# Weight pages of 4608 bytes, with the split weights begun at another offset in each group of 512 columns

## The chip, the cores and the metric

The kernel runs on one core of a Trainium2 chip. The metric is the device time of one execution in microseconds (us). The kernel before was timed twice: 1624.48 and 1625.87 us, median 1625.17 us.

## What is computed

One layer of a streaming encoder on 256 tokens of width 2048, float32 throughout. Cut to what matters here:

```
xn = rms_norm(h)
proj = xn @ w_in            # z_a (u, v), q, c_kv, q_idx, k_idx, w_idx, gates
y_a = spatial_gating_unit(gelu(z_a))
y_b = indexer_sparse_attention(q, rms_norm(c_kv), q_idx, k_idx, w_idx, w_uk, w_uv)
mixed = g_a * (y_a @ w_oa) + g_b * (y_b @ w_ob)
h = h + mixed @ w_out
hn = rms_norm(h)
h = h + (silu(hn @ w_ff_gate) * (hn @ w_ff_up)) @ w_ff_down     # inner width 5632
return rms_norm(h)
```

Nearly all of the work is products of 256 tokens with weight matrices, some 300 MB of weights that are each read once.

## The kernel before, in words

**Weights.** Every weight matrix is cut into groups of 512 columns, and each group into chunks of two k tiles: 128 partitions by 1024 float32 numbers, 512 KB. `wchunk` (line 72) handles one chunk: SyncE (SP) loads it into a page `raw` (line 80), ScalarE (ACT) writes its upper mantissa bits to a page `wh` (line 67), and VectorE (DVE) writes the rest to a page `wl` (line 68). The pool `wp` (line 44) has four pages each of `raw`, `wh` and `wl`, 4096 bytes long in each partition; a chunk's matmuls free its `wh` and `wl` when they are through.

**Products.** A product in float32 is three passes: upper by upper, lower by upper, upper by lower. `nat_group` (line 89, with `mm3` at lines 84 to 87) makes `[tokens, 512]` blocks: the activations are the stationary operand (the weight load, PEld), and 512 columns of `wh` or `wl` stream past them as the moving operand. That is 12 matmuls of 512 columns to a chunk. The groups v, u, g (gates), oa, ob, out, vv, fg, fu and fd are made so: 488 chunks. `tr_group` (line 104, matmuls at lines 117, 119 and 120) has it the other way round: 128x128 pieces of `wh` or `wl` are the stationary operand and 256 tokens move, 24 matmuls to a chunk. The groups qi, q and k are made so: 56 chunks. The first product (kv, before any group) has 16 smaller chunks of 592 columns, read as two halves of 296 columns, b = 0 and b = 1, so that the second half begins 1184 bytes into the page.

**Order.** The groups run one after another in the order of the program: kv, qi0, qi1, v0 to v3, then four times q, k, vv, attention, u and a layer norm; gates and oa, gates and ob, out, and the feed-forward blocks fg and fu with the partial down products fd between them. A last part works from eight chunks of `fd` that stay split on chip (`kept_h`, `kept_l`; they lie in pages of the pool `tp`, not `wp`).

**Other pages.** The pool `np` (line 46) holds 11 pages `[128, 2, 512]` float32, 4096 bytes each: x, v, u, the layer norm's factors `gb`, gates, the residual `h`, the feed-forward's `s` and the final gain `fg` (the tile; the group of that name is the gate half of the feed-forward). A tile takes a page that an earlier tile has left, and the first instruction that writes it waits for the last that read the old one. The loads of `gb` (line 340), `h` (line 457) and `fg` (line 505) stand in SP's queue between the weight loads.

Of the kernel before, what the change touches and what calls it, by code (L numbers as in the profile page):

```python
# [30 lines left out]
KVW = LAT + IDXD + IDXH  # L31
NEG = -1.0e38
MARK = -3.0e38
WARM = 8  # matmuls of zeros that open the clock gate


@with_exitstack
def block_kernel(ctx: ExitStack, tc: tile.TileContext, a, out):
    """Every product against a weight matrix is float32 = three float32r passes: an operand is
    split exactly into h (its upper 12 mantissa bits, rounded) and l (the rest, 12 bits), and  # L40
    h*h + l*h + h*l is accumulated in float32."""
    nc = tc.nc
    const = ctx.enter_context(tc.tile_pool(name="const", bufs=1))
    wp = ctx.enter_context(tc.tile_pool(name="wp", bufs=4))
    tp = ctx.enter_context(tc.tile_pool(name="tp", bufs=24))
    np_ = ctx.enter_context(tc.tile_pool(name="np", bufs=11))
    sp = ctx.enter_context(tc.tile_pool(name="sp", bufs=1))
    acc_p = ctx.enter_context(tc.tile_pool(name="acc", bufs=4, space=bass.MemoryType.PSUM))
    aux_p = ctx.enter_context(tc.tile_pool(name="aux", bufs=4, space=bass.MemoryType.PSUM))
# [7 lines left out]
    def acc_tile(name):  # L57
        return acc_p.tile([P, 512], F32, tag="acc", name=name)
# [2 lines left out]
        return aux_p.tile([P, 512], F32, tag="aux", name=name)  # L61

    def split(h, l, src, scale=None):
        """h + l = src (times a scale per partition), exactly."""
        hf = h.bitcast(F32)
        if scale is None:
            nc.scalar.activation(h, src, AF.Copy)  # L67
            nc.vector.tensor_tensor(l, src, hf, op=ALU.subtract)  # L68
        else:
            nc.scalar.activation(h, src, AF.Copy, scale=scale)  # L70
            nc.vector.scalar_tensor_tensor(l, src, scale, hf, op0=ALU.mult, op1=ALU.subtract)

    def wchunk(src, cols, keep=False):
        raw = wp.tile([P, 1024], F32, tag="raw", name="raw")
        if keep:
            h, l = (t_tile(z).rearrange("p a b -> p (a b)") for z in ("kept_h", "kept_l"))
        else:
            h = wp.tile([P, 1024], F32R, tag="wh", name="wh")
            l = wp.tile([P, 1024], F32R, tag="wl", name="wl")
        nc.sync.dma_start(raw[:, :cols], src)  # L80
        split(h[:, :cols], l[:, :cols], raw[:, :cols])
        return h, l
# [4 lines left out]
        nc.tensor.matmul(o, ll, rh, start=False, stop=stop, **kw)  # L87

    def nat_group(w, ks, x, name):
        """[tokens, 512] blocks of x @ w for both token tiles. w: [chunks, 128, 1024] in DRAM;  # L90
        ks: its k tiles; x(k) -> the k tile's (h, l), [128, 256] each."""
        acc = [acc_tile(f"{name}_{t}") for t in range(2)]
        for c in range(len(ks) // 2):
            wh, wl = wchunk(w[c], 1024)
            for j in range(2):
                i = 2 * c + j
                xh, xl = x(ks[i])
                for t in range(2):
                    s = slice(t * P, (t + 1) * P)
                    mm3(acc[t], xh[:, s], xl[:, s], wh[:, j * 512:(j + 1) * 512],  # L100
                        wl[:, j * 512:(j + 1) * 512], i == 0, i == len(ks) - 1)
        return acc

    def tr_group(w, ks, x, name, bank=acc_tile, beside=None):
        """(x @ w).T for 512 columns of w: two banks of [128 columns, 2, 256 tokens]. beside(c) is
        called after each chunk."""
        acc = [bank(f"{name}_{b}").rearrange("p (c t) -> p c t", c=2) for b in range(2)]
        for c in range(len(ks) // 2):
            wh, wl = wchunk(w[c], 1024)
            for j in range(2):  # L110
                i = 2 * c + j
                xh, xl = x(ks[i])
                for ct in range(4):
                    s = slice(j * 512 + ct * P, j * 512 + (ct + 1) * P)
                    o = acc[ct // 2][:, ct % 2, :]
                    last = i == len(ks) - 1
                    nc.tensor.matmul(o, wh[:, s], xh, start=(i == 0 and ct % 2 == 0), stop=False,  # L117
                                     skip_group_check=True)
                    nc.tensor.matmul(o, wh[:, s], xl, start=False, stop=False, skip_group_check=True)  # L119
                    nc.tensor.matmul(o, wl[:, s], xh, start=False, stop=last, skip_group_check=True)  # L120
            if beside is not None:
                beside(c)
        return acc

    def rsqrt(dst, src, mul, add, m, name):
        """dst = 1 / sqrt(src * mul + add), [128, m]: Newton's steps from the bits' guess, each left
        with a factor (a power of two) that the last product takes out."""
        v = sp.tile([P, m], F32, tag=f"rs_v{m}", name=f"{name}_v", bufs=2)
        y = sp.tile([P, m], F32, tag=f"rs_y{m}", name=f"{name}_y", bufs=2)
        w = sp.tile([P, m], F32, tag=f"rs_w{m}", name=f"{name}_w", bufs=2)  # L130
        nc.vector.tensor_scalar(v, src, mul, add, op0=ALU.mult, op1=ALU.add)
        nc.vector.tensor_scalar(y.bitcast(I32), v.bitcast(I32), -0.5, 1597463007.0,
                                op0=ALU.mult, op1=ALU.add)
        for three in (3.0, 12.0, 768.0):
            if m == 1:
                nc.vector.scalar_tensor_tensor(w, y, y, v, op0=ALU.mult, op1=ALU.mult)
            else:
                nc.vector.tensor_tensor(w, y, y, op=ALU.mult)
                nc.vector.tensor_tensor(w, w, v, op=ALU.mult)
            nc.vector.scalar_tensor_tensor(y, w, three, y, op0=ALU.subtract, op1=ALU.mult)  # L140
        nc.vector.tensor_scalar(dst, y, -1.0 / 8192.0, None, op0=ALU.mult)

    def transposed(src, name, h, l, scale=None):
        """src [128 tokens, 2, 512] -> h, l [128, 4, 256 tokens]."""
        for b in range(2):
            pt = aux_tile(f"{name}_pt{b}").rearrange("p (c t) -> p c t", c=2)
            for c in range(2):
                for t in range(2):
                    ct = 2 * b + c
                    nc.tensor.transpose(pt[:, c, t * P:(t + 1) * P], src[:, t, ct * P:(ct + 1) * P], ident)  # L150
            if scale is None:
                split(h[:, 2 * b:2 * b + 2], l[:, 2 * b:2 * b + 2], pt)
            else:
                for c in range(2):
                    ct = 2 * b + c
                    split(h[:, ct], l[:, ct], pt[:, c], scale=scale[:, ct:ct + 1])

# [1 line left out]
    # while the first loads run: the activation table, and the tensor engine's clock  # L159
    warm = const.tile([P, 512], BF16, name="warm")  # L160
    nc.vector.memset(warm, 0.0)
    table = const.tile([P, 1], BF16, name="table")
# [27 lines left out]
    x_nat = a["x"].rearrange("(t p) (n c) -> n p t c", p=P, c=512)  # L190

    def sumsq(ss, src, n):
        """ss[:, n, t] = the sums of squares of src [128, 2, 512]'s rows."""
        for t in range(2):
            junk = sp.tile([P, 512], BF16, tag="junk", name="junk")
            nc.scalar.activation(junk, src[:, t], AF.Square, accum_out=ss[:, n, t:t + 1])
# [7 lines left out]

    ss1 = sp.tile([P, 4, 2], F32, name="ss1")

# [1 line left out]
    KS = list(range(KT))  # L208
    HW = KVW // 2
    kv = [[acc_tile(f"kv{b}{t}") for t in range(2)] for b in range(2)]  # L210
# [54 lines left out]
    def c_of(k):  # L265
        return cT_h[:, k], cT_l[:, k]

# [1 line left out]
    index_queries(1, acc_tile)  # L269
    cT_h, cT_l = t_tile("cT_h"), t_tile("cT_l")  # L270
    transposed(c_n, "cT", cT_h, cT_l, scale=gkv)
# [19 lines left out]

    for hp in range(8):
        score_pair(hp)
    # keep: 0 where a key is kept, else a large negative; [tile 1's 256 keys | tile 0's 128]
    keep = sp.tile([P, T + P], F32, name="keep")
    for t in (1, 0):
        w = (t + 1) * P
        nc.vector.memset(score[t][0:CHUNK, w - CHUNK:w], NEG)
        for i in range(TOPK // 8):
# [2 lines left out]
            nc.vector.match_replace(score[t], m8, score[t], MARK)  # L302
        nc.vector.tensor_scalar(keep[:, :T] if t else keep[:, T:], score[t], 0.5 * (NEG + MARK), -1.0e30,
                                op0=ALU.is_gt, op1=ALU.mult)
    # r1 * B_HEAD_DIM ** -0.5, for tile 1 and tile 0
    ascale = sp.tile([P, 2], F32, name="ascale")
    for t in range(2):
        nc.vector.tensor_scalar(ascale[:, 1 - t:2 - t], r1[:, t:t + 1], P ** -0.5, None, op0=ALU.mult)

# [1 line left out]
    stats = sp.tile([P, 2, 4, 6], F32, name="stats")  # L311
    v_t, u_t = [], []

# [30 lines left out]
        for j, op in ((0, ALU.mult), (1, ALU.add)):  # L344
            nc.vector.tensor_tensor(v_t[n], v_t[n], gb[:, j:j + 1].to_broadcast([P, 2, 512]), op=op)

# [1 line left out]
    yb = []  # L348

    def attention(n):  # L350
# [49 lines left out]
        u_group(n)  # L400
        layer_norm(n)

# [1 line left out]
    ws = n_tile("ws").rearrange("p a b -> p (a b)").rearrange("p (g q) -> p g q", g=GROUPS)  # L404
    nc.vector.memset(ws[CHUNK:, :, :CHUNK], 0.0)
    nc.sync.dma_start(ws[:CHUNK], a["wsT"][:CHUNK])
# [17 lines left out]
            return h[:, k % 4], l[:, k % 4]  # L424
        return f

# [1 line left out]
    def gate(g):  # L428
        acc = nat_group(a["w_g"][g], KS, x_of, f"g{g}")
        o = n_tile(f"gate{g}")  # L430
# [18 lines left out]
        transposed(mix[n], f"mx{n}", h, l)  # L449
        mx_t.append((h, l))  # L450

# [1 line left out]
    ss2 = sp.tile([P, 4, 2], F32, name="ss2")  # L453
    hn, hT = [], []
    for n in range(4):
# [9 lines left out]
        hT.append((h, l))  # L465
    r2 = row_rstd(ss2, "r2")

# [1 line left out]
    at = []  # L469

    def ff_block(b):
# [13 lines left out]
        for t in range(2):  # L485
            nc.vector.tensor_tensor(hn[n][:, t], acc[t], hn[n][:, t], op=ALU.add)

    # the last block's weights stay split on chip, so that token tile 0 is through before tile 1
    ends = (4, 8, NFB - 1)
    b0 = done = 0  # L490
    kept = []
# [51 lines left out]


def _layout(np, i):
    """The arrays as the program reads them: only cut, transposed and joined."""
    x = np.asarray(i["x"])[0]

    def chunks(w, width=512, per=2):
# [4 lines left out]
    w_in = np.asarray(i["w_in"])[0]  # L554
    cuts = np.cumsum([2 * D, D, LAT, IDXH * IDXD, IDXD, IDXH])
    z, q, c, qi, ki, wi, g = np.split(w_in, cuts, axis=1)
    col = lambda v: np.asarray(v).reshape(-1, P).T  # noqa: E731
    ln = np.stack([np.asarray(i["a_ln_g"])[0].reshape(4, 512), np.asarray(i["a_ln_b"])[0].reshape(4, 512)], 1)
    return {
        "x": x,  # L560
# [38 lines left out]
```

## Time and profile before

| | before |
|---|---|
| runs, us | 1624.48, 1625.87 (median 1625.17) |
| span of the profiled execution, us | 1624.0 |
| TensorE (PE) busy | 1613.2 us, 99% |
| weight loads (PEld) busy | 1358.6 us, 84% |
| VectorE (DVE) busy | 893.8 us, 55% |
| ScalarE (ACT) busy | 742.9 us, 46% |
| DMA, mean | 189 GB/s |

The span goes from the first to the last instruction of the profiled execution; what lies around it, start and end of the program, is not in it. The runs lie 0.5 and 1.9 us above the span. A matmul's busy time is modelled to its end and overlaps the next one's, so that what a matmul costs is read from the distance between two starts, not from its duration.

### The profile page before, as it was taken

Reading aid. Unit: us, or ns where it says so; the run is one execution under the profiler, and the core shown is the slowest. Engines: PE = TensorE matmul, PEld = TensorE weight load, DVE = VectorE, ACT = ScalarE, POOL = GpSimd, SP = SyncE. Lnnn points to the kernel's source line nnn. Section 1 sums busy time; section 2 is a strip of 40 time slices with the busy share of each in tenths; the row PEclk is TensorE's granted clock in tenths of the full one; section 3 lists DMA queues with packets and bytes.
Section 4 is the critical chain, followed back from the end, with each engine's and each line's share of the span. In section 5 each row is a group of like instructions: output and inputs, shape, how many; then the busy total and the mean of one; then the engine's idle time right before and its main releaser. Section 6 shows DMA issues by size and latency. Waiting matters only on the chain.

```text
span 1624.0 us, 20315 instructions
## 1 busy us (share of the span) xinstructions
PE 1613.2 (99%) x7954; PEld 1358.6 (84%) x7954; DVE 893.8 (55%) x1084; ACT 742.9 (46%) x891; POOL 1.6 (0%) x8
## 2 busy tenths in 40 slices
PE   9999999999999999999999999999999999999997
PEld 8988989889788888888888888888888888888886
DVE  5695665565754444555556444455545454554575
ACT  6554464554544444444444444444344444334452
POOL 0000000000000000000000000000000000000000
PEclk9999999999999999999999999999999999999999
DMA  8646555555545555555655555555655555555671
GB/s 302 214 138 201 187 168 182 170 177 175 163 161 192 193 193 194 193 183 196 236 186 185 194 185 190 186 191 186 194 191 192 186 191 188 193 192 194 218 253 59
DMA packets 88128, 307.54 MB, mean 189 GB/s; under 512 B 10272, under 2 KB 10528, under 8 KB 88032
## 3 DMA queue, kind: packets, MB, share of 16 engines
q1 hardware_dynamic: 88032, 306.25, 57.2%
q8 instruction: 62, 1.02, 0.2%
q14 instruction: 34, 0.28, 0.0%
HBM read 304.11 MB, written 2.10 MB: 189 GB/s over the span
## 4 chain that ended last, share of the span: by engine, by line
PE 99%; DMA 0%; DVE 0%; ACT 0%; SPq 0%; issue 0%; ACTq 0%
PE fg L85 5%; PE fg L86 5%; PE fg L87 5%; PE fu L86 5%; PE fu L87 5%; PE fu L85 5%; PE fd L87 4%; PE fd L85 4%; PE fd L86 4%; PE g L86 4%; PE g L85 4%; PE g L87 4%; PE q L120 2%; PE q L119 2%; PE q L117 2%; PE u L87 2%
## 5 line engine op out<-in xcount | busy, mean ns | idle before, releaser
L68 DVE TENSOR_TENSOR wl<-raw,wh 128x1024 fp32r<-128x1024 f32 (+1 forms) x560 | 678.9, 1212 | 668.6 <-ACT wh L67 668.2
L67 ACT ACTIVATE wh<-raw 128x1024 fp32r<-128x1024 f32 (+1 forms) x560 | 587.8, 1050 | 764.9 <-PE fu L87 139.4
L86 PE MATMUL fg<-wl,hh 128*128 128x512 f32 x352 | 137.8, 392 | 0.0
L87 PE MATMUL fg<-wh,hl 128*128 128x512 f32 x352 | 137.7, 391 | 0.0
L85 PE MATMUL fg<-wh,hh 128*128 128x512 f32 x352 | 137.1, 390 | 0.0
L85 PE MATMUL fu<-wh,hh 128*128 128x512 f32 x352 | 136.9, 389 | 0.0
L86 PE MATMUL fu<-wl,hh 128*128 128x512 f32 x352 | 136.9, 389 | 0.0
L87 PE MATMUL fu<-wh,hl 128*128 128x512 f32 x352 | 136.9, 389 | 0.0
L86 PE MATMUL fd<-wl,ah 128*128 128x512 f32 x320 | 124.8, 390 | 0.0
L87 PE MATMUL fd<-wh,al 128*128 128x512 f32 x320 | 124.8, 390 | 0.0
L85 PE MATMUL fd<-wh,ah 128*128 128x512 f32 x320 | 124.6, 389 | 0.0
L87 PE MATMUL g<-wh,xl 128*128 128x512 f32 x256 | 100.9, 394 | 0.0
L85 PE MATMUL g<-wh,xh 128*128 128x512 f32 x256 | 100.7, 393 | 0.0
L86 PE MATMUL g<-wl,xh 128*128 128x512 f32 x256 | 99.9, 390 | 0.0
L85 PEld LDWEIGHTS fu<-wh,hh 128*128 128x128 f32 x352 | 66.1, 188 | 13.7
L86 PEld LDWEIGHTS fu<-wl,hh 128*128 128x128 f32 x352 | 66.1, 188 | 13.7
L87 PEld LDWEIGHTS fu<-wh,hl 128*128 128x128 f32 x352 | 66.1, 188 | 13.7
L85 PEld LDWEIGHTS fg<-wh,hh 128*128 128x128 f32 x352 | 66.1, 188 | 13.5
L86 PEld LDWEIGHTS fg<-wl,hh 128*128 128x128 f32 x352 | 66.1, 188 | 13.4
L87 PEld LDWEIGHTS fg<-wh,hl 128*128 128x128 f32 x352 | 66.2, 188 | 13.2
L120 PE MATMUL q<-xh,wl 128*128 128x256 f32 x256 | 72.4, 283 | 0.0
L119 PE MATMUL q<-xl,wh 128*128 128x256 f32 x256 | 72.4, 283 | 0.0
(220 smaller groups left out, 2722.7 us busy)
## 6 DMA issues: line engine op xcount, KB each, us to landing
raw<-in_w_fg SPq DMA_DIRECT2D x88, 512.0 KB, 3.3
raw<-in_w_fu SPq DMA_DIRECT2D x88, 512.0 KB, 3.3
raw<-in_w_fd SPq DMA_DIRECT2D x88, 512.0 KB, 3.3
raw<-in_w_z SPq DMA_DIRECT2D x64, 512.0 KB, 3.3
raw<-in_w_g SPq DMA_DIRECT2D x64, 512.0 KB, 3.3
raw<-in_w_q SPq DMA_DIRECT2D x32, 512.0 KB, 3.3
raw<-in_w_oa SPq DMA_DIRECT2D x32, 512.0 KB, 3.3
raw<-in_w_ob SPq DMA_DIRECT2D x32, 512.0 KB, 3.3
```

The source lines that it names most:

```text
L67: nc.scalar.activation(h, src, AF.Copy)
L68: nc.vector.tensor_tensor(l, src, hf, op=ALU.subtract)
L85: nc.tensor.matmul(o, lh, rh, start=start, stop=False, **kw)
L86: nc.tensor.matmul(o, lh, rl, start=False, stop=False, **kw)
L87: nc.tensor.matmul(o, ll, rh, start=False, stop=stop, **kw)
L117: nc.tensor.matmul(o, wh[:, s], xh, start=(i == 0 and ct % 2 == 0), stop=False, skip_group_check=True)
L119: nc.tensor.matmul(o, wh[:, s], xl, start=False, stop=False, skip_group_check=True)
L120: nc.tensor.matmul(o, wl[:, s], xh, start=False, stop=last, skip_group_check=True)
```

## The change

The pages `wh` and `wl` grow from 1024 to 1152 numbers (4096 to 4608 bytes), and a group writes and reads its 1024 numbers from an offset on that a table gives by the group's name, 0 to 124 numbers, 0 to 496 bytes. The pool `np` has 10 pages in place of 11, for the room. The pool `wp`'s pages lie at 34720 + 4608 n bytes in each partition where they lay at 34720 + 4096 n, and everything behind them lies 4096 bytes higher, the pool `sp` where it was.

```
-WARM = 8  # matmuls of zeros that open the clock gate
+SHIFT = {f"{z}{i}": s for z, ss in (
+    ("v", (0, 8, 16, 24)), ("u", (32, 40, 48, 56)), ("g", (64, 72, 80, 88, 96, 104, 112, 120)),
+    ("oa", (4, 12, 20, 36)), ("ob", (1, 2, 6, 68)), ("out", (100, 28, 92, 124)), ("q", (8, 16, 32, 64)),
+    ("qi", (24, 48)), ("k", (96, 112, 4, 12)), ("vv", (8, 16, 64, 96)),
+    ("fg", (0, 8, 16, 32, 48, 64, 80, 96, 112, 24, 40)), ("fu", (4, 12, 20, 36, 44, 52, 60, 76, 84, 108, 116)),
+    ("fd", (64, 32, 96, 0))) for i, s in enumerate(ss)}
+WARM = 8
...
-    np_ = ctx.enter_context(tc.tile_pool(name="np", bufs=11))
+    np_ = ctx.enter_context(tc.tile_pool(name="np", bufs=10))
...
+    shift = [0]
+
     def wchunk(src, cols, keep=False):
...
-            h = wp.tile([P, 1024], F32R, tag="wh", name="wh")
-            l = wp.tile([P, 1024], F32R, tag="wl", name="wl")
+            h, l = (wp.tile([P, 1024 + 128], F32R, tag=z, name=z)[:, shift[0]:shift[0] + 1024] for z in ("wh", "wl"))
...
     def nat_group(w, ks, x, name):
...
         acc = [acc_tile(f"{name}_{t}") for t in range(2)]
+        shift[0] = SHIFT.get(name, 0)
...
     def tr_group(w, ks, x, name, bank=acc_tile, beside=None):
...
+        shift[0] = SHIFT.get(name, 0)
         acc = [bank(f"{name}_{b}").rearrange("p (c t) -> p c t", c=2) for b in range(2)]
```

The rest of the diff takes out comments. No instruction is added, taken out or moved: on all five engines the same operations on the same shapes stand in the same order. Tiles of `np` share pages with other earlier tiles than before, and by that seven waits differ: the loads of `gb2`, `h1`, `h3`, `fg0` and `fg1` wait for another (or, `gb2` and `h1`, for some) transpose on TensorE, `h2` for none, and the first gate on ScalarE waits for the load of `gb3`.

By where an offset lies against a grid of 32 bytes, on which every page of the kernel begins, before and after, the groups fall into three kinds. On the grid: v, u, g, q, qi, k0, k1, vv, fg and fd. 16 bytes off it: oa0 to oa3, ob3, out0 to out3, k2, k3, and fu0 to fu10. 4, 8 and 24 bytes off it: ob0, ob1 and ob2.

## Rows read from the trace of the kernel before

**Rows 1.** The page: busy time by engine, and the chain that ended last.

```profile
PE 1613.2 (99%) x7954; PEld 1358.6 (84%) x7954; DVE 893.8 (55%) x1084; ACT 742.9 (46%) x891; POOL 1.6 (0%) x8
...
PE 99%; DMA 0%; DVE 0%; ACT 0%; SPq 0%; issue 0%; ACTq 0%
```

**Rows 2.** Timeline from 1000 us, group fu: start us, us, engine, line, operation.

```profile
1000.28 0.39 PE L86 MATMUL fu<-wl,hh 128*128 128x512 f32 x1
...
1000.51 0.39 PE L87 MATMUL fu<-wh,hl 128*128 128x512 f32 x1
...
1001.62 1.06 ACT L67 ACTIVATE wh<-raw 128x1024 fp32r<-128x1024 f32 x1 [1.66 <-PE fu L87]
...
1002.71 1.23 DVE L68 TENSOR_TENSOR wl<-raw,wh 128x1024 fp32r<-128x1024 f32 x1 [1.49 <-ACT wh L67]
...
1003.00 0.39 PE L86 MATMUL fu<-wl,hh 128*128 128x512 f32 x1
```

**Rows 3.** Timeline of PE from 380 us, group q, 256 moving columns.

```profile
380.04 0.28 PE L119 MATMUL q<-xl,wh 128*128 128x256 f32 x1
...
382.44 0.28 PE L117 MATMUL q<-xh,wh 128*128 128x256 f32 x1
```

**Rows 4.** Timeline of PE from 21 us, product kv, 296 moving columns: one chunk.

```profile
21.05 0.30 PE L87 MATMUL kv<-wh,xl 128*128 128x296 f32 x1
21.19 0.30 PE L85 MATMUL kv<-wh,xh 128*128 128x296 f32 x1
21.33 0.30 PE L86 MATMUL kv<-wl,xh 128*128 128x296 f32 x1
21.47 0.30 PE L87 MATMUL kv<-wh,xl 128*128 128x296 f32 x1
...
22.69 0.30 PE L87 MATMUL kv<-wh,xl 128*128 128x296 f32 x1
```

**Rows 5.** Instructions on the tile fu: duration ns min/median/max, first and last start us.

```profile
L85 PE MATMUL fu<-wh,hh x352: 389/389/389, 906.8 to 1547.7; 128*128 128x512 f32 x176
L86 PE MATMUL fu<-wl,hh x352: 389/389/389, 907.1 to 1547.9; 128*128 128x512 f32 x176
L87 PE MATMUL fu<-wh,hl x352: 389/389/389, 907.3 to 1548.1; 128*128 128x512 f32 x176
```

**Rows 6.** Groups by form: line, engine, operation, shape, count, busy us, mean ns.

```profile
L68 DVE TENSOR_TENSOR wl<-raw,wh 128x1024 fp32r<-128x1024 f32 x544 | 666.5, 1225 | 659.9 <-ACT wh L67 659.5
L67 ACT ACTIVATE wh<-raw 128x1024 fp32r<-128x1024 f32 x544 | 576.6, 1060 | 757.4 <-PE fu L87 139.4 <-PE fg L87 121.6 <-PE fd L87 109.7
...
L68 DVE TENSOR_TENSOR wl<-raw,wh 128x592 fp32r<-128x592 f32 x16 | 12.4, 775 | 8.8 <-ACT wh L67 8.6
L67 ACT ACTIVATE wh<-raw 128x592 fp32r<-128x592 f32 x16 | 11.1, 697 | 7.5 <-DMA raw<-in_w_kv 4.6 <-PE kv L87 1.3 <-DVE wl L68 0.9
```

**Rows 7.** Timeline of SP's queue: loads of h (768 us on), gb2 (362), fg (1524).

```profile
362.20 0.43 SPq L340 DMA_DIRECT2D gb<-in_ln  x1
...
771.59 0.43 SPq L457 DMA_DIRECT2D h<-in_x  x1
...
782.47 0.43 SPq L457 DMA_DIRECT2D h<-in_x  x1
...
1524.11 0.42 SPq L505 DMA_DIRECT2D fg<-in_final_g  x1
...
1526.82 0.42 SPq L505 DMA_DIRECT2D fg<-in_final_g  x1
```

**Rows 8.** Transposes on TensorE by tile: first and last start; and the chain's.

```profile
L150 PE MATMUL cT_pt<-ident,c_n x8: 272/272/273, 79.7 to 80.5; 128*128 128x128 f32 x8
...
L150 PE MATMUL ya_pt<-ident,u x32: 270/272/329, 439.0 to 450.6; 128*128 128x128 f32 x32
...
L150 PE MATMUL mx_pt<-ident,gate x32: 270/273/319, 661.5 to 796.0; 128*128 128x128 f32 x32
...
1284.49 0.65 PE a_pt L150 x6
```

**Rows 9.** The loads of gb, and the gates on ScalarE: ns min/median/max, first and last start.

```profile
L340 SPq DMA_DIRECT2D gb<-in_ln x4: 426/428/432, 234.9 to 425.9; - x4
...
DMA to landing us min/median/max: 4.1/4.4/5.1
...
L432 ACT ACTIVATE gate<-g,r_r x16: 682/690/690, 463.7 to 771.6; 128x512 f32<-128x512 f32 x16
```

## The prediction

> **What bounds the kernel now.** I read the page's busy times first, then the chain that ended last, both in [rows 1]: TensorE is busy 1613.2 of 1624.0 us and the chain is 99% PE. Nothing else stands on the path, so the change can matter in two ways alone: by making TensorE's own work longer or shorter, or by holding an operand back for so long that TensorE runs dry. The timeline comes next, since a matmul's 389 ns of duration overlap the next one's. In the group fu two successive starts are 1000.28 and 1000.51, and the same matmul of the next chunk starts at 1003.00 [rows 2]: 2.72 us for a chunk of 12, or 226.7 ns for each matmul of 512 columns. In the group q, 20 matmuls of 256 columns start within 382.44 - 380.04 = 2.40 us, 120.0 ns each [rows 3]. The difference, 106.7 ns for 256 columns, is 0.417 ns for a column (2.4 GHz, the upper clock level), and 226.7 - 213.3 = 13.3 ns are a fixed part of each matmul. With 488 x 12 = 5856 matmuls at 226.7 ns (1327.6 us) and 56 x 24 = 1344 at 120.0 ns (161.3 us), the products that read `wh` and `wl` pages in groups are 1489 of the 1624 us. One extra column time in each of the 5856 would be 2.4 us, and 2% of the run is 32.5 us. About 2% is what a measurement of this kernel can tell from no change.
>
> Then I look at how far the splits run ahead. ACT's split took 1.06 us and had waited 1.66 us for fu's matmuls, that is for a page to come free; DVE's took 1.23 us and had waited 1.49 us for ACT [rows 2]. Both are done with a chunk within 2.72 us and wait for TensorE, not TensorE for them. With four pages, the page that a chunk frees is needed again three chunks later: 3 x 2.72 = 8.16 us, of which the two splits take 1.06 + 1.23 = 2.29. Some 5.9 us are cover.
>
> **The change part by part.** *Instructions.* None is added, removed or moved, and SP's queue issues the same loads in the same order. This costs nothing unless a single instruction takes another time at its new address.
>
> *One page fewer in the pool np.* Seven waits differ; one is gone, and each new one is over long before its instruction's turn. The load of gb2 now waits for a transpose of c_n, the last of which started at 80.5 us [rows 8]; it was issued at 362.20 [rows 7]. The load of h1 waits for a transpose of u (last start 450.6) and was issued at 771.59; that of h3 waits for the first block of the merged gates (661.5 and on) and was issued at 782.47. The two loads of fg wait for transposes of the feed-forward blocks 5 and 6, of which the later is the one at 1284.49, and were issued at 1524.11 and 1526.82. The first gate waits for the load of gb3, issued at 425.9 and landed at most 5.1 us later, and starts at 463.7 [rows 9]. The narrowest of these has 30 us to spare, so no weight load behind such a wait in SP's queue is late, and the cost is 0. If that cover were gone, a wait would hold the weight loads behind it, and TensorE would only feel what goes beyond the some 8 us of chunks that lie ready.
>
> *The splits at shifted addresses.* ACT took 1060 ns for 1024 numbers and 697 ns for 592, 0.84 ns each; DVE 1225 and 775 ns, 1.04 ns each [rows 6]. Both are slopes of one number at a time, and a stream that handles single 4-byte numbers has no larger unit that an offset of whole numbers could split. No row shows such a write off the 32-byte grid, so I bound it: from below 0, from above a split twice as long on both engines, 2.12 and 2.45 us. Each is still under the 2.72 us that TensorE needs for the chunk, and 4.57 us for the pair is under 8.16. I take 0, and 0 on the path at either end, with a little at the top of the range for DVE's other work.
>
> *The matmuls at shifted addresses.* This is the term that decides, as it lies on the path. 24 chunks of nat_group (ob0 to ob2) read at starts 4, 8 and 24 bytes off the grid: 288 matmuls. 160 chunks (oa, ob3, out, fu) read 16 bytes off it: 1920 matmuls. The others stay on the grid. Two rows speak on how TensorE takes an address. In a chunk of kv, six matmuls read at the page's start and six from 1184 bytes on, which is 37 x 32 and so moves the start against any grid of 64 bytes or more; all 12 take 22.69 - 21.05 = 1.64 us, 136.7 ns each, and the single steps are 0.13 to 0.14 us without a pattern of six and six [rows 4]. By the slope above, 296 columns and the fixed part make 123.3 + 13.3 = 136.7 ns: neither start costs more. And in fu, 3 x 352 matmuls, over four pages of each kind, two halves of a page and 32 places of the stationary operand, with ACT and DVE writing other pages most of the time, have one duration, 389 ns least and most [rows 5]. If one address clashed with another, or with a write, this row would be spread. So at steps of 32 bytes the price is 0, by rows. For starts within 32 bytes the trace has no row. The bounds are: below, the fixed part goes, -13.3 ns; above, every column is fetched twice, +213.3 ns. I take 0, since the nearest row is [rows 4], where a shift costs nothing, and the stream is again paced at one column of 4 bytes for each 0.417 ns.
>
> The Trainium skill speaks against the change here: its page "SBUF — State Buffer", section "Specifications (TRN2)", says that the memory is read in lines of 16 bytes and that each cross to a new line pays a penalty. Only ob0 to ob2 start inside such a line; 512 numbers then touch 129 lines in place of 128. Even if the whole 226.7 ns were the reading of 128 lines, the extra one would be 1.8 ns, an estimate, and 288 of them 0.5 us; the sum would be 1625.7 instead of 1625.2. No run here shows it yet. The same page's section "Operand start alignment" lets a float32 operand start at any multiple of 4 bytes, but says that this is about legality and that the runs behind it timed nothing, so it settles no price.
>
> *Weight loads at shifted addresses.* In tr_group it is the stationary operand that shifts; q, qi, k0 and k1 stay on the grid, and k2 and k3 (4 chunks, 96 loads) lie 16 bytes off. Twice the 120.0 ns step would be 96 x 120.0 = 11.5 us; I take 0 for the reason above.
>
> *Sum.* 1624.0 us of span + 0 + 0 + 0 + 0, and the 0.5 to 1.9 us that the runs lie above the span, whose middle is 1.2: 1625.2 us, the median of the runs shown.
>
> **The rivals.** *Starts within 32 bytes fetch twice (slower).* Where an operand begins off the unit in which TensorE reads, each step needs two fetches, and the moving stream takes a second pass, +213.3 ns. If the unit is 16 bytes, it hits ob0 to ob2 alone: 288 x 213.3 = 61.4 us, 1686.6 us, 3.8% slower. If it is 32 bytes, it hits 2208 matmuls: 471 us, 2096 us. It decides (2%) from 32.5 / 288 = 113 ns for the first, from 32.5 / 2208 = 14.7 ns for the second. For it: no row shows such a start. Against it: [rows 4] at the next coarser step. 5% together, most of it the first.
>
> *The fixed part doubles off the grid (a small loss).* If 13.3 ns are a start-up that an odd start pays twice, 2208 x 13.3 = 29.4 us, 1654.6 us: 1.8%, just within. Against it: in [rows 4] the fixed part is the same at both starts. 3%, some of which goes beyond 2%.
>
> *The fixed part shrinks (faster).* The pages begin 32 bytes off a grid of 64, so offsets of 8, 24, 40 ... numbers put 90 chunks (v1, v3, u1, u3, four of g, vv0, fg1, fg9, fg10) onto it. Losing the 13.3 ns there gives 1080 x 13.3 = 14.4 us, 1610.8 us, within 2%. [Rows 4] speak against it: b = 1 begins on that grid and shows the full 13.3 ns. 2%; for over 2% all 5424 shifted matmuls would have to lose 6 ns each. 1%.
>
> *The change doesn't do what it says*: if the pages kept their addresses, the time is the forecast's; it is part of that case.
>
> **How the numbers follow.** No change in time: 89%. Fetched twice: 5%. Fixed part doubles: 3%. Faster in either way: 3%. The range takes the first case with small prices that the rows could not show: two column times won in all 5424 shifted matmuls (-4.5 us) to four column times lost (+9.0 us): 1620 to 1634 us; the others stay outside, 11%. Faster by over 2%: 1%, rounded up to 2 for what I have not thought of. Slower by over 2%: the 5% and half of the 3%, some 7. Within: 91%.
>
> **What would show it.** After the change the tile rows of ob, oa and fu should still have one duration of 389 ns, and chunks of ob0 to ob2 should be 2.72 us apart; ACT's and DVE's splits should stay at 1060 and 1225 ns; the loads of h and fg should be issued at the same times. I am wrong if ob0 to ob2 last longer than ob3, or oa, out and fu longer than g and fg; if DVE's splits grow so far that PE's idle time names them; or if every group changes alike, which would be the pages' new distance and not the offsets.

## The result, and the profile after

The changed kernel took 1649.7 us (median; 1649.16 and 1650.23) against 1625.17: a ratio of 1.0153 with a 95% interval from 1.0124 to 1.0183. It is 24.5 us slower, under 2%, but clear of noise and outside the range of the prediction.

The page of the changed kernel shows where the time is: in TensorE's own work, and nowhere else.

```profile
PE 1637.9 (99%) x7954; PEld 1358.0 (82%) x7954; DVE 893.6 (54%) x1084; ACT 743.1 (45%) x891; POOL 1.6 (0%) x8
...
PE 99%; DMA 0%; DVE 0%; ACT 0%; SPq 0%; ACTq 0%; issue 0%
```

Against [rows 1] PE's busy time grew by 24.7 us with the same 7954 matmuls, the other engines' times stand still, and the chain is still 99% PE. The groups by form (line, engine, operation, shape, count, busy us, mean ns) say that the splits keep their prices at the new addresses, which answers to [rows 6]:

```profile
L76 DVE TENSOR_TENSOR wl<-raw,wh 128x1024 fp32r<-128x1024 f32 x544 | 666.2, 1225 | 683.3 <-ACT wh L75 683.1
L75 ACT ACTIVATE wh<-raw 128x1024 fp32r<-128x1024 f32 x544 | 576.5, 1060 | 778.7 <-PE fu L96 146.5 <-PE fg L96 125.4 <-PE fd L96 111.1
```

The instructions on the tile fu (ns least/median/most, first and last start), which answer to [rows 5], where all three had 389/389/389:

```profile
L94 PE MATMUL fu<-wh,hh x352: 387/396/403, 917.6 to 1571.6; 128*128 128x512 f32 x176
L95 PE MATMUL fu<-wl,hh x352: 388/396/403, 917.8 to 1571.8; 128*128 128x512 f32 x176
L96 PE MATMUL fu<-wh,hl x352: 390/396/403, 918.1 to 1572.1; 128*128 128x512 f32 x176
```

A single duration has become a spread, and its middle is 7 ns higher. The timeline of group ob0 (offset 1 number) gives the distance of two starts that are 12 matmuls apart:

```profile
658.12 0.40 PE L94 MATMUL ob<-wh,ybh 128*128 128x512 f32 x1
...
660.98 0.40 PE L94 MATMUL ob<-wh,ybh 128*128 128x512 f32 x1
```

2.86 us, 238 ns a matmul in place of 226.7. Read the same way over a whole group, from its first start to its last (fu0: 917.60 to 939.61 us for 95 steps, 231.7 ns; before 906.83 to 928.36, 226.6 ns), every group gets a price by its offset. Where transposes stand among a group's first matmuls, the price is the mean of the steps that they don't interrupt, less the same mean before. That mean takes in the steps before the group settles and reads up to 1 ns low: the group out3 settles at steps of 233 and 234 ns, 6.7 above, and the table has 6.0 for it.

| offset in numbers | groups | ns a matmul above 226.7 |
|---|---|---|
| 0 and 64 | v0, g0, fg0, fg5, fd0, fd3 | 0 (within 0.5) |
| 4 and 68 | fu0, oa0, ob3 | 5.0 |
| 8 and 72 | v1, fg1, g1 | 6.3 to 6.7 |
| 12 and 76 | oa1, fu1, fu7 | 6.5 to 6.6 |
| 16 and 80 | v2, fg2, fg6, g2 | 1.9 to 2.3 |
| 20 and 84 | oa2, fu2, fu8 | 4.4 to 4.5 |
| 32 and 96 | fg3, fg7, g4, fd1, fd2 | 5.2 to 6.7 |
| 48 and 112 | fg4, fg8, g6 | 6.2 to 6.5 |
| 52 and 116 | fu5, fu10 | 8.0 |
| 60 and 124 | fu6; out3 | 9.8; 6.0 |
| 1, 2, 6 | ob0, ob1, ob2 | 11.1, 6.0, 6.7 |

The price repeats after 64 numbers, 256 bytes, and has nothing to do with the 16 or 32 bytes on which the prediction sorted the groups: 8 numbers, on the grid of 32 bytes, cost more than 4, off it. In the groups of 256 columns, where the weights are stationary, the shift has the other sign: q1 (16) took 117.8 ns in place of 120.0, qi0 (24) 117.3, while q3 (64) kept 119.9. Summed over the starts, the groups of 512 columns lost 28.5 us and those of 256 columns won 2.2. The span grew by 24.4 us (1624.0 to 1648.5); the 1.9 us between are what the interrupted steps, the steps between groups and the attention took less.

### The profile page after: what moved, and what is told of

Its sections match the earlier page's. It is cut to its first block, busy times and chain, and to the rows that moved or that the text cites. A ratio compares the mean times of both kernels' runs of the same rounds, so it can differ in the third digit from the quotient of the medians.

```text
span 1648.5 us, 20317 instructions
## 1 busy us (share of the span) xinstructions
PE 1637.9 (99%) x7954; PEld 1358.0 (82%) x7954; DVE 893.6 (54%) x1084; ACT 743.1 (45%) x891; POOL 1.6 (0%) x8
## 4 chain that ended last, share of the span: by engine, by line
PE 99%; DMA 0%; DVE 0%; ACT 0%; SPq 0%; ACTq 0%; issue 0%
PE fu L96 5%; PE fu L95 5%; PE fu L94 5%; PE fg L96 5%; PE fg L94 5%; PE fg L95 5%; PE fd L94 4%; PE fd L95 4%; PE fd L96 4%; PE g L96 4%; PE g L95 4%; PE g L94 4%; PE q L130 2%; PE q L128 2%; PE q L131 2%; PE ob L96 2%
## 5 line engine op out<-in xcount | busy, mean ns | idle before, releaser
L96 PEld LDWEIGHTS fg<-wh,hl 128*128 128x128 f32 x352 | 66.2, 188 | 14.7
L94 PEld LDWEIGHTS fg<-wh,hh 128*128 128x128 f32 x352 | 66.1, 188 | 14.7
```

Of the source, the lines that this page charges most:

```text
L94: nc.tensor.matmul(o, lh, rh, start=start, stop=False, **kw)
```

## The experiments

Theory A: the price hangs on the distance between the moving and the stationary operand, counted within 256 bytes. In the trace the two overlap: the next matmul's weight load runs beside the columns of the present one (PEld is busy 84% of the span and PE 99%, [rows 1]). Theory B: it hangs on the moving operand's own start. Rivals: the pages' new distance, the smaller pool, and the writes of the splits.

**Pages of 4608 bytes and the pool of 10 alone.** Both groups' functions set

```
-        shift[0] = SHIFT.get(name, 0)
+        shift[0] = 0
```

> The pages of 4608 bytes and the pool of 10, with every offset at 0: weights and activations begin at the same place of a stretch of 256 bytes, as before. Theory A (the offset of the moving operand against the stationary operand costs, as the two are read at once): 226.7 ns for each matmul of 512 columns, 120.0 of 256, 1625 us. Theory B (the moving operand's own start costs, wherever the other lies): the same, 1625 us. Rival C (the pages' distance of 4608 bytes, or the tenth page of the other pool, costs): 1648 to 1651 us, the changed kernel's time.

Measured 1624.99 us (10 runs; ratio 1.0003, interval 0.9994 to 1.0013), and on the tile fu

```profile
L94 PE MATMUL fu<-wh,hh x352: 389/389/389, 907.0 to 1547.8; 128*128 128x512 f32 x176
L95 PE MATMUL fu<-wl,hh x352: 389/389/389, 907.2 to 1548.1; 128*128 128x512 f32 x176
```

The distance of 4608 bytes (18 x 256) and the changed waits cost nothing; rival C falls, and the offsets are all of it.

**Everything 32 bytes later.** One small constant ahead of all pages of the kernel before:

```
+    pad = const.tile([P, 8], F32, name="pad")
+    nc.vector.memset(pad, 0.0)
```

> The kernel before with 32 bytes ahead of every page, so that weights, activations and all else lie 32 bytes later and nothing moves against anything. Theory A (offset between the two operands): 226.7 ns a matmul, 1625 us. Theory B (the moving operand's own start): every group as the groups with an offset of 8 numbers in the changed kernel, some 233.4 ns, so 5856 x 6.7 ns = 39 us more, less some 2 us in the groups of 256 columns: about 1662 us.

Measured 1625.9 us in one run (span 1624.1), where 13 runs of the kernel before took 1624.11 to 1625.97, and fu unchanged:

```profile
L85 PE MATMUL fu<-wh,hh x352: 389/389/389, 907.0 to 1547.8; 128*128 128x512 f32 x176
```

Here every weight begins where it began with the offset 8, at 6.3 to 6.7 ns in the changed kernel, and pays nothing; the activations moved along. Theory B falls.

**The activations alone 32 bytes later.** The same 32 bytes, but in a pool of their own between the weights' and the activations' pools:

```
     wp = ctx.enter_context(tc.tile_pool(name="wp", bufs=4))
+    pads = ctx.enter_context(tc.tile_pool(name="pads", bufs=1))
...
+    pad = pads.tile([P, 8], F32, name="pad")
+    nc.vector.memset(pad, 0.0)
```

> The kernel before with 32 bytes between the weights' pages and the activations' pages: the weights lie where they lay, the activations 32 bytes later, so the weights begin 8 numbers earlier against them, which is 56 in a period of 64. Theory A (offset between the two operands): as the group with an offset of 120 numbers in the changed kernel, some 232.7 ns instead of 226.7, so 5856 x 6 ns = 35 us more, less some 2 us in the groups of 256 columns: about 1658 us. Theory B (the moving operand's own start): the groups of 512 columns keep 226.7 ns, 1625 us; in the groups of 256 columns, where the activations move, 120 ns changes.

Measured 1654.6 us in one run (span 1652.8), with no weight page at another address than before:

```profile
L86 PE MATMUL fu<-wh,hh x352: 395/396/396, 917.4 to 1575.3; 128*128 128x512 f32 x176
L87 PE MATMUL fu<-wl,hh x352: 395/396/396, 917.7 to 1575.6; 128*128 128x512 f32 x176
L88 PE MATMUL fu<-wh,hl x352: 395/396/396, 917.9 to 1575.8; 128*128 128x512 f32 x176
```

A loss of 6.7 ns stands in nearly every group of 512 columns (36.2 us over the starts), and the groups of 256 columns win 3.2 ns each (4.3 us). Theory A holds. The distance can be checked in the groups of 256 columns: the weights now begin 56 numbers on in the period of 64, and q's steps are 116.7 ns, as in qi0 at offset 56 in the next run (116.7), and not 118.4 as in q0 at offset 8 in the changed kernel. This run also clears the splits' writes: they go to the same pages at the same places as before, and in fu nothing but the weight loads touches the activations.

**The curve, and one page shifted alone.** The changed kernel with another table, and in group fu a pair of offsets, one for `wh` and one for `wl`:

```
...
+    ("v", (60, 1, 16, 17)), ("g", (59, 57, 55, 54, 50, 46, 42, 38)),
+    ("oa", (60, 52, 1, 63)), ("ob", (60, 1, 16, 63)), ("out", (60, 1, 16, 63)), ("q", (20, 22, 26, 28)),
+    ("qi", (56, 60)), ("k", (1, 2, 40, 44)),
+    ("fg", (60, 62, 63, 61, 58, 3, 5, 10, 14, 18, 34)), ("fd", (22, 30, 33, 47))) for i, s in enumerate(ss)}
+SHIFT |= {f"fu{i}": s for i, s in enumerate(((8, 0), (0, 8), (16, 0), (0, 16), (32, 0), (0, 32), (4, 0), (0, 4), (1, 0), (0, 1), 60))}
...
```

> The changed kernel with another table: offsets 60, 1 and 16 in several groups, and others that the table did not have (odd ones, 63, 62, 54, 50 ...); in the group fu an offset for the upper parts' page alone or for the lower parts' page alone. Theory A and theory B: the same offset costs the same in every group (60: +9.8 ns, 1: +11, 16: +2), apart from what the pattern of the two streams settles into, and 63 as much as 1 if only the distance matters. With one page shifted alone, theory A in the form that each matmul meets the next weight load: the loss stands at the matmuls that stream the shifted page, so the upper page alone (two of three passes) gives about two thirds and the lower page alone one third of the loss of both. Rival D (ScalarE's and VectorE's writes meet TensorE's reads): the loss follows the writes in time and not the pass.

Measured 1656.77 us in one run. By the starts: 1 costs 10.5 to 11.2 ns in v, oa, ob and out alike, 16 costs 2.2 to 2.4, 63 only 0.7 to 1.3, 59 about 1.2, 3 2.2, 5 12.1, 17 13.0, 61 12.6. So distances close by differ by a factor of ten, 63 (one less than 0) is not 1 (one more), and nothing lies under 0. 60 gave two answers: 9.8 to 10.0 ns in oa0, ob0 and fu10, 6.2 to 6.3 in out0 and fg0 (6.7 once they settle).

The part of the expectation on single pages missed. The timeline's first and last start of fu0 (upper page at 8 alone) and fu1 (lower page alone):

```profile
918.70 0.40 PE L94 MATMUL fu<-wh,hh 128*128 128x512 f32 x1
...
940.67 0.39 PE L96 MATMUL fu<-wh,hl 128*128 128x512 f32 x1
...
964.09 0.40 PE L94 MATMUL fu<-wh,hh 128*128 128x512 f32 x1
...
986.26 0.39 PE L96 MATMUL fu<-wh,hl 128*128 128x512 f32 x1
```

95 steps in 21.97 us are 4.6 ns above 226.7, and in 22.17 us 6.7 ns. Two of three passes shifted cost less than one, and both pages at 8 cost 6.3 to 6.7, not the sum. With 16 the parts cost 6.7 and 5.3 and both together 2.3. So the price isn't a sum over passes. That each matmul starts where the delay of the one before has left it would fit, but no run shows it, and which weight load meets which columns couldn't be read from this.

**Offsets where the activations move.** Offsets in q (3, 5, 6, 7), qi (2, 62) and k (10, 18, 34, 58) only, all groups of 512 columns at 0.

> Offsets only in the groups where the weights are the stationary operand and 256 columns of activations move (q, qi, k), other ones than so far: 3, 5, 6, 7, 2, 62, 10, 18, 34, 58; all groups of 512 columns at 0. Theory A (offset between the two operands): 226.7 ns in every group of 512 columns, as before, and under 120 ns in most of the shifted groups, 115.7 at 2 as in the short group k1 of the curve; about 1344 x 3 ns = 4 us less, 1620 to 1623 us. Theory B (the moving operand's own start): the activations lie where they lay, so 120 ns and 1625 us.

Measured 1621.21 us in one run, its kernel before 1625.69. Steps by the starts, 120.0 ns without offset: 2 gave 115.7, 3 and 7 116.7, 62 117.7, 34 117.9, 18 118.4, 58 118.3, 6 118.7, 10 119.2, and 5 120.0. The 512-column groups kept 226.7. As theory A has it; only 5 stood still.

**All groups of 512 columns at 33.**

```
+SHIFT = {f"{z}{i}": 33 for z, n in (
+    ("v", 4), ("u", 4), ("g", 8), ("oa", 4), ("ob", 4), ("out", 4), ("vv", 4), ("fg", 11), ("fu", 11),
+    ("fd", 4)) for i in range(n)}
```

> All 488 chunks of 512 columns at one offset, 33 numbers (132 bytes), the dearest of the curve with +13.2 ns a matmul; the groups of 256 columns at 0. Theory A, with the price a property of the offset and adding up over the matmuls: 5856 x 13.2 = 77 us more, about 1701 us. If the loss in the curve hung on the mixture of groups (what a group leaves to the next), or were hidden where nothing else waits: clearly less.

Measured 1678.63 us in one run: 53 us more, not 77. The tile rows of ob (three groups at the dearer price) and fu:

```profile
L91 PEld LDWEIGHTS fu<-wh,hh x352: 187/188/188, 933.3 to 1598.6; 128*128 128x128 f32 x176
L91 PE MATMUL fu<-wh,hh x352: 397/398/400, 933.5 to 1598.8; 128*128 128x512 f32 x176
...
L91 PEld LDWEIGHTS ob<-wh,ybh x128: 187/192/193, 651.1 to 813.8; 128*128 128x128 f32 x128
L91 PE MATMUL ob<-wh,ybh x128: 397/404/404, 651.3 to 814.1; 128*128 128x512 f32 x128
```

The same offset has two prices, 9.5 ns in fu and most others and 13.3 in g5 to g7, ob1 to ob3, out0 to out2 and part of u: durations of 398 and 404 ns. The weight loads differ too, 188 ns in fu and 192 in ob. In ob1 all steps are 240 ns; in fu they repeat a pattern from 231 to 239. A group falls into one rhythm and keeps it, some into the next groups; in u, which attention interrupts, both occur, and a stretch changes from one to the other only after a gap. The loss is real in every group, but a price read from one group is good only to such a factor.

**Pages of 4128 bytes.** The kernel before with eight numbers more to a page, and no offset in it:

```
-            h = wp.tile([P, 1024], F32R, tag="wh", name="wh")
-            l = wp.tile([P, 1024], F32R, tag="wl", name="wl")
+            h = wp.tile([P, 1024 + 8], F32R, tag="wh", name="wh")[:, :1024]
+            l = wp.tile([P, 1024 + 8], F32R, tag="wl", name="wl")[:, :1024]
```

> The kernel before with wh and wl pages of 4128 bytes in place of 4096, no offset in any page and nothing else changed (the other pool keeps 11 pages). The pages then begin at 0, 8, 16 and 24 numbers (wh) and 32, 40, 48 and 56 (wl) against the activations in a period of 64. Theory A (offset between the two operands, whatever makes it): the mean of the curve at these eight places, some 5 ns a matmul, 5856 x 5 = 30 us more, about 1655 us, less 2 to 4 us in the groups of 256 columns. Rival (it is the offset within a page that costs, or the change of offset from group to group): 1625 us.

Measured 1650.07 us in one run (span 1648.3), with fu as spread as after the change:

```profile
L85 PE MATMUL fu<-wh,hh x352: 387/394/398, 916.0 to 1570.9; 128*128 128x512 f32 x176
L86 PE MATMUL fu<-wl,hh x352: 391/395/398, 916.3 to 1571.2; 128*128 128x512 f32 x176
```

The groups of 512 columns lost 29.8 us, 5.1 ns a matmul, and those of 256 won 3.1. The distance counts, whatever makes it; 32 bytes of padding to a page cost as much as the whole table.

**Offset 2 in q, qi and k alone**, in pages of 4352 bytes (17 x 256), 10 pages in `np`:

```
+SHIFT = {f"{z}{i}": 2 for z, n in (("q", 4), ("qi", 2), ("k", 4)) for i in range(n)}
...
+            h, l = (wp.tile([P, 1024 + 64], F32R, tag=z, name=z)[:, shift[0]:shift[0] + 1024] for z in ("wh", "wl"))
```

> Offset 2 numbers (8 bytes) in the groups q, qi and k alone, where the weights are the stationary operand, pages of 4352 bytes (a multiple of 256); every group of 512 columns at 0. Theory A with the price by offset as measured: 115.7 ns in place of 120.0 in 1344 matmuls, 5.7 us less, 226.7 ns kept elsewhere: 1619 to 1620 us, a ratio of 0.9965 to the kernel before. If the gain is given back somewhere (at the groups' ends, in attention): 1625 us.

Measured 1618.86 us (5 runs) against 1624.80: ratio 0.9963, interval 0.9950 to 0.9977, faster than both kernels. The groups of q before, and in this kernel:

```profile
L120 PE MATMUL q<-xh,wl 128*128 128x256 f32 x256 | 72.4, 283 | 0.0
L119 PE MATMUL q<-xl,wh 128*128 128x256 f32 x256 | 72.4, 283 | 0.0
```

```profile
L125 PE MATMUL q<-xl,wh 128*128 128x256 f32 x256 | 71.3, 279 | 0.0
...
L126 PE MATMUL q<-xh,wl 128*128 128x256 f32 x256 | 71.0, 277 | 0.0
```

The starts give 5.8 us won in 1344 matmuls, 4.3 ns each, and fu and ob stay at 389/389/389. The weight loads in q, before and in this kernel (ns least/median/most):

```profile
L117 PEld LDWEIGHTS q<-xh,wh x256: 187/192/192, 176.5 to 390.2; 128*128 128x128 f32 x128
```

```profile
L123 PEld LDWEIGHTS q<-xh,wh x256: 187/188/188, 173.8 to 383.6; 128*128 128x128 f32 x128
```

The load went from 192 to 188 ns, about what the step won. The gain arrives at the end.

## Why the prediction was wrong

*What bounds the kernel, the sizes of a step, and the cover of the splits* held: PE stayed the chain, 226.7 and 120.0 ns are the steps at offset 0, ACT and DVE took 1060 and 1225 ns again. *The pool of 10* held too: the kernel with pages and pool alone stands at 1.0003 of before.

*The matmuls at shifted addresses* is the step that failed, in its own words: "So at steps of 32 bytes the price is 0, by rows. For starts within 32 bytes the trace has no row." Both prices, the 0 for the grid and the 0 then taken within it, were wrong. The groups on the 32-byte grid, priced at 0, lost 14.7 of the 28.5 us; those 16 bytes off lost 11.5 and ob0 to ob2, the ones feared most, 2.3. Three readings led there.

First, the question was put to one operand. The weights' address was asked about, and the stationary operand was taken as a bystander, though PEld is 84% busy beside PE in [rows 1]. The runs with 32 bytes show that the distance between the two is what costs.

Second, [rows 5] was used as a test that it couldn't be. One duration over "four pages of each kind, two halves of a page and 32 places of the stationary operand" would show a clash only if these places differ within 256 bytes. They don't: pages lie 4096 bytes apart, halves 2048, stationary pieces 512. The row shows one distance, 0, measured 1056 times.

Third, [rows 4] was the one row of before with another distance (1184 bytes are 296 numbers, 40 in a period of 64), and it was read by its mean. 136.7 ns is what the slope gives, but it came out of times rounded to 0.01 us; at nanoseconds the chunk takes 1633 ns, 136.1 each. And the row's steps of 0.13 and 0.14 us were no rounding: at nanoseconds they run from 131 to 140 and repeat after 12 matmuls, while fu's steps are 226 and 227 throughout. The rows by tile of kv before the change, which the prediction doesn't use, say the same:

```profile
L85 PE MATMUL kv<-wh,xh x64: 294/300/613, 5.4 to 33.0; 128*128 128x296 f32 x64
L86 PE MATMUL kv<-wl,xh x64: 294/298/448, 5.8 to 33.2; 128*128 128x296 f32 x64
L87 PE MATMUL kv<-wh,xl x64: 294/300/448, 6.6 to 33.3; 128*128 128x296 f32 x64
```

The long ends come from the product's first 15 matmuls, 247 ns apart; but least and median differ by 4 to 6 ns, where fu's do not differ at all. A mean that fits was taken as the absence of a mechanism; here dearer and cheaper steps cancel.

The rivals had the sign and missed the place. "Starts within 32 bytes fetch twice" would have put the loss into ob0 to ob2 at 213 ns each; they pay 11.1, 6.0 and 6.7. "The fixed part doubles off the grid" came near in size (1654.6 us against 1649.7) by a wrong count: not 13.3 ns on 2208 matmuls, but 1.9 to 11.1 on nearly all that were shifted off a multiple of 256 bytes, on the grid or not. "The fixed part shrinks" was looked for in the groups of 512 columns and occurs in those of 256, where 120.0 became 117.3 to 118.7. The weight loads at shifted addresses, taken at 0 with 11.5 us as the bound on the slow side, won 2.2 us.

The Trainium skill, "TensorE: Matmul & The Clock Gate", section "Step-by-step: what each phase is for", says that TensorE has two independent read ports, so that loading the next weights takes no read bandwidth from the running matmul. If that means that the addresses of the two reads don't matter to each other, the runs differ: with nothing else changed than the distance of the two operands, a matmul of 512 columns took 226.7 to 240.0 ns, one of 256 columns 115.7 to 120.0. The prediction also weighed the lines of 16 bytes of the Trainium skill, "SBUF — State Buffer", section "Specifications (TRN2)". Crossing such lines doesn't give the pattern: an offset of 8 numbers, two whole lines, cost 6.3 to 6.7 ns.

What stays open: what in the chip has the period of 256 bytes, and which weight load meets which columns. That it is the distance that costs is shown. That the two reads hinder each other is argued from it; the nearest to it in the traces are the weight loads, at 192 ns in q at distance 0 and in ob at 33, and at 188 ns in q at 2 and in fu at 33. Most groups of 512 columns don't show it: ob in the changed kernel lost 5.0 to 11.1 ns a matmul with weight loads of 188 ns (median) as before.

## What to carry to other kernels

Keep the moving and the stationary operand of long streams of float32 matmuls with 512 columns at the same place of a 256-byte stretch, and give pages that alternate a length of a multiple of 256 bytes; 32 bytes of padding cost this kernel 1.6%. Other operand types and shapes were not tried. Where 256 columns move, try a small distance: 8 bytes won 4.3 of 120 ns. And before a row is used to exclude an address effect, work out whether its addresses differ at all, and look at the spread of its durations, not at their mean.

## What the runs showed that was not expected

- A distance of 0 is the best that was found for 512 columns, where 41 others cost 0.7 to 13.3 ns, and among the worst for 256, where 22 of 26 others won 0.8 to 4.3 ns and four (5, 26, 28 and 40) nothing.
- The same distance can have two prices. 33 numbers cost 9.5 ns in most groups and 13.3 in some, 60 cost 6.3 or 9.8; within a group the steps settle into a pattern that repeats.
- Close distances differ by much: 59 cost 1.2 ns and 57 10.0, 63 cost 0.7 to 1.3 and 61 12.6.
